# Side work of the DeltaNet projections: three places per product block instead of two, and the block inverses on one engine each

## The chip, the cores and the metric

One Trainium2 chip, and of it one core. The time is what the device takes for one execution, in microseconds. The kernel before ran three times: 3624.55, 3621.60 and 3624.28 us, median 3624.28.

## The reference, cut to what matters

A two-layer backbone over 1024 latent tokens and 256 context tokens, width 1024, float32. Layer 0 is an mLSTM and S5 mixer, layer 1 a bidirectional gated DeltaNet with 8 heads of 128; each is followed by a SwiGLU block. The change touches layer 1's mixer alone:

```
pc, pl = split(hc @ w_in), split(hl @ w_in)            # q, k, v, z and gates, 8 heads
qkv = silu(depthwise_conv3x3(...))                      # over a 64-column grid; the context is one row
q, k = l2norm(q) * scale, l2norm(k)
A   = strict_lower((k * beta) @ k.T * gamma)            # per chunk and head
sol = triangular_solve(A + I, [v * beta, k * beta * exp(G)])
attn = (q @ k.T) * gamma
S, (v_new, o_inter) = scan(step, 0, ...)                # the recurrence over the chunks
o = o_inter + attn @ v_new                              # both directions are added
y = rmsnorm(o) * silu(z) @ w_out
```

The kernel works with chunks of 128 tokens (10 of them: 2 context, 8 latent). The triangular solve becomes an explicit inverse of each 128x128 matrix: first of its 32x32 diagonal blocks, then of 64x64 and 128x128.

## The kernel before, in words

Every dense product runs three times in reduced precision (`mm3`, lines 124 to 126: high times high, high times low, low times high). `dense` makes one product block: 8 steps over the contraction, so 24 matmuls into one accumulator tile `pd`, for 256 (context, chunk 0) or 512 columns (chunks 1 and 2).

Layer 1's mixer has two stages. In the first, `layer1` calls `gdn_project` for the heads 0 to 7. For one head it makes the block of K (chunks 0, 1, 2), of Q (1, 2), for heads 0 to 5 that of the output gate z (`gdn_gate`, chunks 1 and 2), and of V (0, 1, 2). `conv_input` copies each product into an image, and `conv_block` does the 3x3 convolution there: line 1693 on ScalarE, lines 1695 on VectorE (8 taps of 751 ns for 512 columns), then the SiLU (lines 1697, 1698). The first K and Q blocks were made earlier. The gate blocks of heads 6 and 7 come last (`hw`).

**The side work of a head** is the generator `gdn_keys(h)`, started before the head's V block. It runs in pieces, from one `yield` to the next, and `pull(n)` runs n pieces at that place of the program. Its pieces: transposes of K (3) and Q (2) to token order with sums of squares (`to_tokens`: line 1710 on TensorE, 1713 and 1718 on ScalarE); the logarithms of the norms (line 1780 and `log_half`, lines 1530 to 1544, some 17 small VectorE steps that each need the one before) and from them the row factors `ei` (lines 1785 on VectorE, 1789 on ScalarE), written under `high_priority`; `K1` empty pieces; then the row parts `d_pr` (line 1821: TensorE transposes `ei`; lines 1822 to 1825: VectorE makes `rows` of it); `Y2` = 2 empty pieces; exponentials times Q (2 pieces, `d_qE`: TensorE 1843, ScalarE 1845, GpSimd 1847, stored by a DMA); then for three groups of chunks the decay factors (TensorE 1855 and 1857, ScalarE 1860) and the products K·K and K·Q (TensorE 1866 and 1878, GpSimd 1869, VectorE 1870 and 1881; 6 pieces), stored by DMAs; then V's transposes (3). Those are 18 pieces and K1 empty ones, and K0 more for head 0. With two places in a product block (one in its middle, one at its end) a head has 20 places: V 6, K 6, Q 4, gate 4. `set_side` first runs what is left of the old generator. For head 7 the pieces wait differently (L1, Y1, L2, K2).

**The 32x32 inverses** are `gdn_base(h0, nh)`: a load from `bl_dr`, 30 elimination steps, a masking at the end (lines 1929 to 1934) and a store to `bo_dr`. Each step has two halves, one per triangle, and each half is a product into `b_t` (lines 1920, 1924) and a sum into `b_x` (line 1926). The half r = 0 is on VectorE, r = 1 on GpSimd. It runs three times: heads 0 to 2 (written from head 4 on, one step per unit of the convolution), heads 3 to 5 (written after head 7), heads 6 and 7 (written in the second stage, heads 2 to 4). There is one buffer `b_x`.

In the second stage, `gdn_heads` runs the recurrence head by head (`gdn_recur`: TensorE 2073, 2081, 2104, VectorE 2075 and 2109, ScalarE 2085), with the next head's larger inverse (`gdn_inverse`) between its steps.

What sets the order: inside the mixer TensorE's instructions stay in program order (`in_pe_order`). Those of VectorE, ScalarE, GpSimd and the DMA issues are put in order by the framework, from a simulated timeline with priorities by program order (`high_priority` raises one by 400), and each engine then runs its own queue strictly in that order. So work that is written late but needs nothing late may stand early in a queue.

Of the kernel before, what the change touches and what calls it, by code (L numbers as in the profile page):

```python
# [16 lines left out]
P = 128  # L17
D = 1024
# [8 lines left out]
FFN = 2816  # L27
HP = 400
Y1, Y2 = 6, 2
K0, K1, K2 = 3, 3, 3  # L30
R0, R1, R2, R3 = 3,1,1,2
F1, F2 = 20,8
L1, L2 = 4,2
# [9 lines left out]
class Kernel:  # L43
# [84 lines left out]
    def dense(self, w, rhs, kb, n, c0=0, order=None, mid=0):  # L128


        ps = self.psd.tile([P, 512], F32, name="pd")
        for j, k in enumerate(order or range(kb)):
            if mid and j == kb // 2:
                self.pull(mid)
            self.mm3(ps[:, :n], (w[0][:, k, c0:c0 + P], w[1][:, k, c0:c0 + P]), rhs(k), j == 0, j == kb - 1)
        return ps[:, :n]
# [1518 lines left out]
    def conv_input(self, hs, w, img, chunks, mid=0):  # L1655

        nc = self.nc
        g, l = img
        for ci in chunks:
            t0, n = CHUNKS[ci]  # L1660
            ps = self.dense(w, lambda k: (hs[ci][0][:, k], hs[ci][1][:, k]), KB, n, mid=mid)
            if ci == 0:
                nc.scalar.copy(out=l[:, 1:1 + NCTX], in_=ps)
            else:
                r0 = 1 + (t0 - NCTX) // 64
                nc.scalar.copy(out=g[:, r0:r0 + n // 64, 1:65], in_=ps.rearrange("p (r c) -> p r c", c=64))
            self.pull(mid)

    def conv_block(self, hs, w0, blk, out, with_ctx, pool, mid=1):

        nc = self.nc
        g, l = img = self.img[self.nimg % 2]
        self.nimg += 1
        if blk not in self.early:
            w = self.load_w(self.ins["od_w_in"][0], 0, KB, w0)
            self.conv_input(hs, w, img, (0, 1, 2) if with_ctx else (1, 2), mid=mid)

        wc = lambda i: self.wcv[:, blk, i:i + 1]
        off = NCTX if with_ctx else 0
        units = [(out[:, 0:NCTX], (NCTX,), {i: l[:, i - 3:i - 3 + NCTX] for i in (4, 3, 5)})] if with_ctx else []  # L1680
        for hf in range(2):
            taps = {}
            for i in (4, 0, 1, 2, 3, 5, 6, 7, 8):
                dy, dx = divmod(i, 3)
                taps[i] = g[:, 8 * hf + dy:8 * hf + dy + 8, dx:dx + 64]
            units.append((out[:, off + 512 * hf:off + 512 * hf + 512], (8, 64), taps))
        for o, shape, taps in units:
            n = o.shape[-1]
            acc = self.psc.tile([P, 512], F32, name="cv_acc", tag="pc")[:, :n]
            a = acc.rearrange("p (r c) -> p r c", c=64) if len(shape) == 2 else acc  # L1690
            for i, src in taps.items():
                if i == 4:
                    nc.scalar.activation(out=a, in_=src, func=AF.Copy, scale=wc(4))  # L1693
                else:
                    nc.vector.scalar_tensor_tensor(out=a, in0=src, scalar=wc(i), in1=a, op0=ALU.mult, op1=ALU.add)  # L1695
            th = pool.tile([P, 512], F32, name="cv_th")
            nc.scalar.activation(out=th[:, :n], in_=acc, func=AF.Tanh, scale=0.5)
            nc.vector.scalar_tensor_tensor(out=o, in0=th[:, :n], scalar=1.0, in1=acc, op0=ALU.add, op1=ALU.mult)
            next(self.base, None)
# [21 lines left out]
    def gdn_gate(self, hs, hw, ci, qp, n=1):  # L1721

        nc = self.nc
        t0, nt = CHUNKS[ci]
        for h, w in hw:
            ps = self.dense(w, lambda k: (hs[ci][0][:, k], hs[ci][1][:, k]), KB, nt, mid=n)
            self.pull(n)
            zz = qp.tile([P, 512], F32, name="cv_th")
            nc.scalar.activation(out=zz, in_=ps, func=AF.Tanh, scale=0.5)
            nc.vector.scalar_tensor_tensor(out=zz, in0=zz, scalar=1.0, in1=ps, op0=ALU.add, op1=ALU.mult)  # L1730
            nc.sync.dma_start(out=self.z_dr[h, :, t0 - NCTX:t0 - NCTX + nt], in_=zz)
# [3 lines left out]

    LATE = 6

    def gdn_project(self, hs, h, tp, qp, kp):

        last = h == 7  # L1740
        kqv = [None] * 3
        def start():
            self.set_side(self.gdn_keys(h, kqv, kp, qp))
            self.pull()
        kT = tp.tile([P, T], F32, name="d_fT", bufs=3)
        self.conv_block(hs, D + h * P, 8 + h, kT, True, qp, 2 if last else 1)
        kqv[0] = kT
        self.nc.sync.dma_start(out=self.k_dr[h], in_=kT)
        qT = tp.tile([P, NLAT], F32, name="d_qT", bufs=2)
        if last:  # L1750
            start()
        self.conv_block(hs, h * P, h, qT, False, qp)
        kqv[1] = qT
        if h < self.LATE:
            w = self.gdn_gate_w(h)
            for ci in (1, 2):
                self.gdn_gate(hs, [(h, w)], ci, qp)
        vT = tp.tile([P, T], F32, name="d_fT", bufs=3)
        if not last:
            start()  # L1760
        self.conv_block(hs, 2 * D + h * P, 16 + h, vT, True, qp)
        kqv[2] = vT

# [139 lines left out]
            nc.gpsimd.affine_select(out=fb, in_=fb, pattern=[[-s, 32], [s, 32]], compare_op=ALU.is_ge, fill=0.0, base=0, channel_multiplier=0)  # L1903
        nc.gpsimd.tensor_copy(self.bm, f)

    def gdn_base(self, h0, nh, pool):

        nc = self.nc
        x = self.bx[:, 0]
# [1 line left out]
            nc.sync.dma_start(out=x[32 * b:32 * b + 10 * nh], in_=self.bl_dr[b, h0:h0 + nh].rearrange("h c j i -> (h c) j i"))  # L1911
        yield
        for j in range(1, 31):
            for r, e in ((0, nc.vector), (1, nc.gpsimd)):
                t = pool.tile([P, 256], F32, name=f"b_t{r}")
                m = 31 - j
                tv = t[:, :j * m]
                if r == 0:
                    tv = tv.rearrange("p (k i) -> p k i", i=m)
                    e.tensor_tensor(out=tv, in0=x[:, 0:j, j:j + 1].to_broadcast([P, j, m]), in1=x[:, j:j + 1, j + 1:].to_broadcast([P, j, m]), op=ALU.mult)  # L1920
                    d = x[:, 0:j, j + 1:]
                else:
                    tv = tv.rearrange("p (i k) -> p i k", k=j)
                    e.tensor_tensor(out=tv, in0=x[:, j + 1:, j:j + 1].to_broadcast([P, m, j]), in1=x[:, j:j + 1, 0:j].to_broadcast([P, m, j]), op=ALU.mult)
                    d = x[:, j + 1:, 0:j]
                e.tensor_tensor(out=d, in0=d, in1=tv, op=ALU.add)
            yield
# [224 lines left out]
    def layer1(self):  # L2152
# [40 lines left out]
        with s1:  # L2193
# [11 lines left out]
                self.ei3.append(t)  # L2205
            self.base = iter(())
            for h in range(8):
                if h == 4:
                    self.base = self.gdn_base(0, 3, bp)
                self.gdn_project(hs, h, tp, qp, kp)  # L2210
            for _ in self.base:
                pass
            self.base = self.gdn_base(3, 3, bp)
            next(self.base)
            hw = [(h, self.gdn_gate_w(h)) for h in range(self.LATE, 8)]
            self.gdn_gate(hs, hw, 1, qp, G1)
            self.gdn_places()
# [22 lines left out]
    def gdn_heads(self, bp, sb):  # L2240
# [16 lines left out]
        for h in range(8):  # L2257
            with self.tc.high_priority(offset=HP):
                next(finish, None)
            if h < 7:  # L2260
                with self.tc.issue_after(self.blocks_dma.ins):
                    tn = self.gdn_load(h + 1, (d0, d1)[(h + 1) % 2])
                if h == 1:
                    for _ in base:
                        pass
                    base = self.gdn_base(6, 2, bp)
                    with self.tc.issue_after(tn["dma"].ins):
                        next(base)
                inv = self.gdn_inverse(h + 1, tn)
# [120 lines left out]
```

## Time and profile before

| | |
|---|---|
| median of 3 runs | 3624.28 us |
| profiled execution | 3625.0 us, of it the traced span 3623.3 us |
| busy in the span | TensorE 3368.1, weight loads 2788.7, VectorE 1904.1, ScalarE 1003.9, GpSimd 954.2 us |
| mean granted TensorE clock | 0.966 |
| first stage (projections) | about 1875 to 2430 us of the span |
| second stage (recurrence) | about 2470 to 2780 us |

"Busy" of TensorE is modelled and holds no idle time; time at half clock counts as busy. PE is TensorE, PEld its weight loads, DVE VectorE, ACT ScalarE, POOL GpSimd. Outside the two stages, layer 0 and the SwiGLU blocks fill the span.

### The profile page before, as it was taken

What the parts mean: (1) busy time and instruction counts of PE and PEld (TensorE: products, weight loads), DVE (VectorE), ACT (ScalarE), POOL (GpSimd) and SP (SyncE); (2) the same over time, 40 slices, a digit from 0 to 9 for tenths busy, and PEclk for the clock granted to TensorE, in tenths of its full rate; (3) what the DMA queues carried; (4) which work ended last, traced back from release to release, by engine and by line L of the source; (5) the groups of instructions that cost most, each with busy time, mean ns of one, the idle gap of its engine ahead of it and who ended that gap; (6) DMA issues with size and microseconds to landing.
All of it is one profiled execution on the core that took longest, in us unless ns stands there. A gap on an engine that the chain in (4) does not pass through costs nothing. (4 is left out here: it accounts for less than half of the span.)

```text
span 3623.3 us, 48343 instructions
## 1 busy us (share of the span) xinstructions
PE 3368.1 (93%) x18527; PEld 2788.7 (77%) x18527; DVE 1904.1 (53%) x4084; ACT 1003.9 (28%) x2409; POOL 954.2 (26%) x783
## 2 busy tenths in 40 slices
PE   6999978999999999999988979788899999999998
PEld 4787667886777778888777767567897788888888
DVE  6659967444333333333467797885754432222224
ACT  3221135331111111111244535443444211111112
POOL 1111124141111111111342352444543222222223
PEclk7999989999999999999999989899999999999999
DMA  7553575512222221111123333246553011111111
GB/s 241 130 168 122 165 213 147 178 59 89 92 81 75 77 76 53 41 35 41 59 63 95 114 117 119 89 131 205 154 183 134 24 45 52 48 48 51 43 53 65
DMA packets 396828, 360.31 MB, mean 99 GB/s; under 512 B 104763, under 2 KB 329755, under 8 KB 396086
## 3 DMA queue, kind: packets, MB, share of 16 engines
q1 hardware_dynamic: 396598, 357.23, 31.9%
q8 instruction: 146, 2.39, 0.3%
q14 instruction: 84, 0.69, 0.1%
HBM read 258.92 MB, written 96.75 MB: 98 GB/s over the span
## 5 line engine op out<-in xcount | busy, mean ns | idle before, releaser
L124 PE MATMUL pd<-hh,w_hi 128*128 128x512 f32 (+1 forms) x3064 | 1156.0, 378 | 3.9 <-ACT hh L284 3.3
L125 PE MATMUL pd<-hl,w_hi 128*128 128x512 f32 (+1 forms) x3064 | 1137.7, 371 | 3.0 <-DVE hl L276 2.9
L126 PE MATMUL pd<-hh,w_lo 128*128 128x512 f32 (+1 forms) x3064 | 1131.8, 371 | 1.6 <-POOL w_lo L118 1.5
L118 POOL TENSOR_TENSOR w_lo<-w_raw,w_hi 128x1024 fp32r<-128x1024 f32 (+2 forms) x205 | 479.2, 2338 | 2004.3 <-ACT w_hi L117 1930.8
L124 PEld LDWEIGHTS pd<-hh,w_hi 128*128 128x128 f32 x3064 | 588.5, 192 | 116.6 <-issue 8.6
L126 PEld LDWEIGHTS pd<-hh,w_lo 128*128 128x128 f32 x3064 | 586.8, 192 | 108.2 <-issue 2.9
L125 PEld LDWEIGHTS pd<-hl,w_hi 128*128 128x128 f32 x3064 | 588.3, 192 | 103.1 <-DVE hl L276 6.0
L117 ACT CAST w_hi<-w_raw 128x1024 fp32r<-128x1024 f32 (+2 forms) x205 | 207.6, 1012 | 964.4 <-PE pd L125 750.1
L1337 DVE SCALAR_TENSOR_TENSOR x<-pd,mod,x 128x512 f32<-128x512 f32 (+1 forms) x408 | 267.5, 670 | 267.1 <-PE pd L126 266.8
L1325 DVE TENSOR_TENSOR ntmp<-ntmp,pd 128x512 f32<-128x512 f32 (+1 forms) x110 | 69.8, 634 | 508.2 <-PE pd L126 507.9
L124 PE MATMUL pd<-g_hi,w_hi 128*128 128x512 f32 (+1 forms) x844 | 314.3, 373 | 0.6 <-DVE x L1337 0.6
L125 PE MATMUL pd<-g_lo,w_hi 128*128 128x512 f32 (+1 forms) x844 | 307.1, 364 | 0.0
L126 PE MATMUL pd<-g_hi,w_lo 128*128 128x512 f32 (+1 forms) x844 | 302.4, 364 | 0.6 <-POOL w_lo L118 0.6
L1695 DVE SCALAR_TENSOR_TENSOR cv_acc<-img,wcv,cv_acc 128x512 f32<-128x512 f32 x384 | 278.6, 751 | 39.6 <-ACT cv_acc L1693 26.8
L1324 DVE SCALAR_TENSOR_TENSOR ntmp<-ntmp,pd 128x512 f32<-128x512 f32 (+1 forms) x110 | 69.7, 634 | 269.9 <-ACT ntmp L1323 268.2
L124 PEld LDWEIGHTS pd<-g_hi,w_hi 128*128 128x128 f32 x844 | 159.2, 189 | 49.3 <-issue 21.4
L1326 ACT ACTIVATE g_hi<-ntmp 128x512 fp32r<-128x512 f32 (+1 forms) x110 | 64.7, 588 | 441.9 <-DVE ntmp L1325 441.5
L126 PEld LDWEIGHTS pd<-g_hi,w_lo 128*128 128x128 f32 x844 | 158.3, 188 | 28.7 <-issue 2.1
L125 PEld LDWEIGHTS pd<-g_lo,w_hi 128*128 128x128 f32 x844 | 159.4, 189 | 23.1
L1327 DVE SCALAR_TENSOR_TENSOR g_lo<-ntmp,g_hi 128x512 fp32r<-128x512 f32 (+1 forms) x110 | 139.7, 1270 | 68.2 <-ACT g_hi L1326 68.2
L245 POOL TENSOR_TENSOR nacc<-nacc,ntmp 128x256 f32<-128x256 f32 (+1 forms) x72 | 74.5, 1040 | 125.2 <-ACT ntmp L241 123.6
L189 PE MATMUL a_ps<-a_raw,svec 128*32 128x256 f32 x768 | 84.4, 435 | 19.3 <-DMA a_raw<-in_ada_w_dram 19.3
(542 smaller groups left out, 4535.6 us busy)
## 6 DMA issues: line engine op xcount, KB each, us to landing
w_raw<-in_ffn_w_dram SPq DMA_DIRECT2D x106, 512.0 KB
a_raw<-in_ada_w_dram SPq DMA_DIRECT2D x96, 512.0 KB
w_raw<-in_od_w_in_dram SPq DMA_DIRECT2D x32, 512.0 KB
w_raw<-in_ffn_w_dram SPq DMA_DIRECT2D x32, 384.0 KB
w_raw<-in_ev_w_in_dram SPq DMA_DIRECT2D x20, 512.0 KB
x_dr<-x SPq DMA_DIRECT2D x4, 2048.0 KB
p_dr<-mp_t SPq DMA_DIRECT2D x32, 256.0 KB
x<-x_dr SPq DMA_DIRECT2D x16, 512.0 KB
```

The source lines that it names most:

```text
L117: nc.scalar.copy(out=hi, in_=raw)
L118: self.w_lo_engine.tensor_tensor(out=lo, in0=raw, in1=hi.bitcast(F32), op=ALU.subtract)
L124: mm(ps, lh, rh, start=first, stop=False)
L125: mm(ps, lh, rl, start=False, stop=False)
L126: mm(ps, ll, rh, start=False, stop=last)
L189: nc.tensor.matmul(ps[32 * j:32 * j + 32, :256], self.svec[:, k], raw[:, j * 256:(j + 1) * 256], start=(k == 0), stop=(k == KB - 1), tile_ ...
L245: nc.gpsimd.tensor_tensor(out=acc, in0=acc, in1=sq, op=ALU.add)
L1324: nc.vector.scalar_tensor_tensor(out=th[:, :n], in0=th[:, :n], scalar=1.0, in1=p1, op0=ALU.add, op1=ALU.mult)
L1325: nc.vector.tensor_tensor(out=th[:, :n], in0=th[:, :n], in1=p3, op=ALU.mult)
L1327: nc.vector.scalar_tensor_tensor(out=gl[:, t0:t0 + n], in0=th[:, :n], scalar=0.5, in1=gh[:, t0:t0 + n].bitcast(F32), op0=ALU.mult, op1=ALU ...
L1337: nc.vector.scalar_tensor_tensor(out=xd, in0=ps, scalar=g, in1=xd, op0=ALU.mult, op1=ALU.add)
L1695: nc.vector.scalar_tensor_tensor(out=a, in0=src, scalar=wc(i), in1=a, op0=ALU.mult, op1=ALU.add)
```

## The change

- `K0, K1` go from 3, 3 to 4, 7.
- `dense` takes a tuple of steps at which to pull a piece; for a tuple of m places, m - 1 more are pulled at the block's end. With (3, 5) a product block has three places: before step 3, before step 5, at its end. K, Q, gate and V of the heads take it. The K block of head 7 takes (2, 3, 5, 6): seven pieces per product block (four before).
- `gdn_base` gets its engine: heads 0 to 2 and 3 to 5 wholly on GpSimd, heads 6 and 7 wholly on VectorE. The masking at the end stays on VectorE.
- The inverses of heads 0 to 2 are written from the V block of head 3 on (before: from head 4), those of heads 3 to 5 from the V block of head 7 on (before: after it), with two steps at each gate block of heads 6 and 7.

```diff
--- before.py
+++ after.py
@@ -27,7 +27,7 @@
 FFN = 2816
 HP = 400
 Y1, Y2 = 6, 2
-K0, K1, K2 = 3, 3, 3
+K0, K1, K2 = 4, 7, 3
 R0, R1, R2, R3 = 3,1,1,2
 F1, F2 = 20,8
 L1, L2 = 4,2
@@ -130,7 +130,9 @@
 
         ps = self.psd.tile([P, 512], F32, name="pd")
         for j, k in enumerate(order or range(kb)):
-            if mid and j == kb // 2:
+            if isinstance(mid, tuple):
+                self.pull(mid.count(j))
+            elif mid and j == kb // 2:
                 self.pull(mid)
             self.mm3(ps[:, :n], (w[0][:, k, c0:c0 + P], w[1][:, k, c0:c0 + P]), rhs(k), j == 0, j == kb - 1)
         return ps[:, :n]
@@ -1664,9 +1666,9 @@
             else:
                 r0 = 1 + (t0 - NCTX) // 64
                 nc.scalar.copy(out=g[:, r0:r0 + n // 64, 1:65], in_=ps.rearrange("p (r c) -> p r c", c=64))
-            self.pull(mid)
-
-    def conv_block(self, hs, w0, blk, out, with_ctx, pool, mid=1):
+            self.pull(len(mid) - 1 if isinstance(mid, tuple) else mid)
+
+    def conv_block(self, hs, w0, blk, out, with_ctx, pool, mid=(3, 5)):
 
         nc = self.nc
         g, l = img = self.img[self.nimg % 2]
@@ -1724,7 +1726,10 @@
         t0, nt = CHUNKS[ci]
         for h, w in hw:
             ps = self.dense(w, lambda k: (hs[ci][0][:, k], hs[ci][1][:, k]), KB, nt, mid=n)
-            self.pull(n)
+            self.pull(len(n) - 1 if isinstance(n, tuple) else n)
+            if h >= self.LATE:
+                next(self.base, None)
+                next(self.base, None)
             zz = qp.tile([P, 512], F32, name="cv_th")
             nc.scalar.activation(out=zz, in_=ps, func=AF.Tanh, scale=0.5)
             nc.vector.scalar_tensor_tensor(out=zz, in0=zz, scalar=1.0, in1=ps, op0=ALU.add, op1=ALU.mult)
@@ -1735,7 +1740,7 @@
 
     LATE = 6
 
-    def gdn_project(self, hs, h, tp, qp, kp):
+    def gdn_project(self, hs, h, tp, qp, kp, bp):
 
         last = h == 7
         kqv = [None] * 3
@@ -1743,7 +1748,7 @@
             self.set_side(self.gdn_keys(h, kqv, kp, qp))
             self.pull()
         kT = tp.tile([P, T], F32, name="d_fT", bufs=3)
-        self.conv_block(hs, D + h * P, 8 + h, kT, True, qp, 2 if last else 1)
+        self.conv_block(hs, D + h * P, 8 + h, kT, True, qp, (2, 3, 5, 6) if last else (3, 5))
         kqv[0] = kT
         self.nc.sync.dma_start(out=self.k_dr[h], in_=kT)
         qT = tp.tile([P, NLAT], F32, name="d_qT", bufs=2)
@@ -1754,10 +1759,15 @@
         if h < self.LATE:
             w = self.gdn_gate_w(h)
             for ci in (1, 2):
-                self.gdn_gate(hs, [(h, w)], ci, qp)
+                self.gdn_gate(hs, [(h, w)], ci, qp, (3, 5))
         vT = tp.tile([P, T], F32, name="d_fT", bufs=3)
         if not last:
             start()
+
+        if h in (3, 7):
+            for _ in self.base:
+                pass
+            self.base = self.gdn_base(0 if h == 3 else 3, 3, bp, self.nc.gpsimd)
         self.conv_block(hs, 2 * D + h * P, 16 + h, vT, True, qp)
         kqv[2] = vT
 
@@ -1903,7 +1913,7 @@
             nc.gpsimd.affine_select(out=fb, in_=fb, pattern=[[-s, 32], [s, 32]], compare_op=ALU.is_ge, fill=0.0, base=0, channel_multiplier=0)
         nc.gpsimd.tensor_copy(self.bm, f)
 
-    def gdn_base(self, h0, nh, pool):
+    def gdn_base(self, h0, nh, pool, e):
 
         nc = self.nc
         x = self.bx[:, 0]
@@ -1911,9 +1921,9 @@
             nc.sync.dma_start(out=x[32 * b:32 * b + 10 * nh], in_=self.bl_dr[b, h0:h0 + nh].rearrange("h c j i -> (h c) j i"))
         yield
         for j in range(1, 31):
-            for r, e in ((0, nc.vector), (1, nc.gpsimd)):
+            m = 31 - j
+            for r in range(2):
                 t = pool.tile([P, 256], F32, name=f"b_t{r}")
-                m = 31 - j
                 tv = t[:, :j * m]
                 if r == 0:
                     tv = tv.rearrange("p (k i) -> p k i", i=m)
@@ -2205,13 +2215,7 @@
                 self.ei3.append(t)
             self.base = iter(())
             for h in range(8):
-                if h == 4:
-                    self.base = self.gdn_base(0, 3, bp)
-                self.gdn_project(hs, h, tp, qp, kp)
-            for _ in self.base:
-                pass
-            self.base = self.gdn_base(3, 3, bp)
-            next(self.base)
+                self.gdn_project(hs, h, tp, qp, kp, bp)
             hw = [(h, self.gdn_gate_w(h)) for h in range(self.LATE, 8)]
             self.gdn_gate(hs, hw, 1, qp, G1)
             self.gdn_places()
@@ -2263,7 +2267,7 @@
                 if h == 1:
                     for _ in base:
                         pass
-                    base = self.gdn_base(6, 2, bp)
+                    base = self.gdn_base(6, 2, bp, nc.vector)
                     with self.tc.issue_after(tn["dma"].ins):
                         next(base)
                 inv = self.gdn_inverse(h + 1, tn)
```

## Rows read from the trace of the kernel before

**Rows 1.** Two stretches: busy PE, PEld, DVE, ACT, POOL (count); clock, DMA share, GB/s.
```profile
1880.00:2440.00 560.00, 465.90 (x2526) 385.97 (x2527) 467.80 (x861) 263.02 (x775) 219.34 (x225) 0.92 0.35 109
...
2515.00:2590.00 75.00, 62.53 (x468) 57.41 (x468) 62.81 (x157) 25.61 (x93) 53.44 (x82) 0.98 0.40 114
```

**Rows 2.** Waits of TensorE, 1880:2095, 2095:2430, 2340:2430: us in total, times, longest.
```profile
PE d_pr L1821 <- ACT ei L1789: 15.8, 3, 6.0
...
PE d_pr L1821 <- ACT ei L1789: 47.8, 4, 20.9
...
PE d_pk L1866 <- DVE d_ca L1870: 3.9, 1, 3.9
PE d_pE L1843 <- DVE rows L1825: 1.3, 1, 1.3
```

**Rows 3.** Timeline of TensorE, head 2: start us, us, instruction [idle before it <- releaser].
```profile
2036.11 0.60 PE L1710 MATMUL tt_ps<-ident,d_qT 128*128 128x128 f32 x4
...
2044.79 0.28 PE L126 MATMUL pd<-hh,w_lo 128*128 128x256 f32 x1
2049.99 0.48 PE L1821 MATMUL d_pr<-ident,ei 128*128 128x128 f32 x1 [4.92 <-ACT ei L1789]
```

**Rows 4.** The same view's columns as rows 1, stretches after waits.
```profile
2345.80:2362.70 16.90, 11.49 (x72) 9.00 (x71) 16.26 (x25) 7.87 (x21) 14.24 (x16) 1.00 0.12 47
2050.10:2055.50 5.40, 5.40 (x14) 4.24 (x15) 5.21 (x12) 0.55 (x2) 0.00 (x0) 0.50 0.00 0
2134.20:2137.50 3.30, 3.29 (x9) 2.61 (x10) 3.18 (x10) 1.07 (x4) 0.20 (x1) 0.50 0.00 0
```

**Rows 5.** Timeline of VectorE, head 2: the logarithms' first and last steps.
```profile
2038.88 0.18 DVE L1780 TENSOR_SCALAR d_ss<-d_ss 128x18 f32<-128x18 f32 x1 [0.33 <-ACT tt_sq L1718]
...
2049.00 0.21 DVE L1785 TENSOR_TENSOR d_e<-dg_pre,d_lkq 128x60 f32<-128x60 f32 x1
```

**Rows 6.** Timelines of TensorE and VectorE, head 3.
```profile
2104.31 0.60 PE L1710 MATMUL tt_ps<-ident,d_qT 128*128 128x128 f32 x4
...
2134.21 0.48 PE L1821 MATMUL d_pr<-ident,ei 128*128 128x128 f32 x1 [20.94 <-ACT ei L1789]
...
2111.84 0.62 DVE L1780 TENSOR_SCALAR d_ss<-d_ss 128x18 f32<-128x18 f32 x1
```

**Rows 7.** Busy time while head 3's logarithms run: all engines; line 1920; line 1926.
```profile
2111.80:2133.80 22.00, 1.47 (x13) 1.27 (x11) 22.00 (x49) 2.14 (x4) 19.73 (x32) 0.62 0.09 24
...
2111.80:2133.80 22.00, 3.94 (x6) 0.62 0.09 24
...
2111.80:2133.80 22.00, 2.57 (x7) 8.94 (x16) 0.62 0.09 24
```

**Rows 8.** Timeline of TensorE, head 6.
```profile
2342.60 0.48 PE L1821 MATMUL d_pr<-ident,ei 128*128 128x128 f32 x1 [16.99 <-ACT ei L1789]
```

**Rows 9.** Instructions of tile b_x: duration ns min/median/max, first and last start, forms.
```profile
L1920 DVE TENSOR_TENSOR b_t<-b_x x90: 191/392/2462, 2093.5 to 2563.5; 128x30 f32<-128x30 f32 x6, 128x58 f32<-128x58 f32 x6, 128x84 f32<-128x84 f32 x6, 128x108 f32<-128x108 f32 x6
L1924 POOL TENSOR_TENSOR b_t<-b_x x90: 235/539/781, 2093.5 to 2580.5; 128x30 f32<-128x30 f32 x6, 128x58 f32<-128x58 f32 x6, 128x84 f32<-128x84 f32 x6, 128x108 f32<-128x108 f32 x6
L1926 DVE TENSOR_TENSOR b_x<-b_x,b_t x90: 190/390/1410, 2093.7 to 2563.7; 128x30 f32<-128x30 f32 x6, 128x58 f32<-128x58 f32 x6, 128x84 f32<-128x84 f32 x6, 128x108 f32<-128x108 f32 x6
L1926 POOL TENSOR_TENSOR b_x<-b_x,b_t x90: 249/578/927, 2093.9 to 2580.8; 128x30 f32<-128x30 f32 x6, 128x58 f32<-128x58 f32 x6, 128x84 f32<-128x84 f32 x6, 128x108 f32<-128x108 f32 x6
```

**Rows 10.** Lines 1869, 1860 in 1880:2440, columns as rows 9; one ScalarE wait.
```profile
L1869 POOL TENSOR_TENSOR d_ca<-d_e,d_e x23: 722/1272/1408, 1938.7 to 2438.9; 128x512 f32<-128x512 f32 x15, 128x256 f32<-128x256 f32 x8
...
L1860 ACT ACTIVATE d_e<-d_pe,d_e x152: 349/380/429, 1936.7 to 2438.4; 128x128 f32<-128x128 f32 x152
...
ACT d_qE L1845 <- DMA q_dr<-d_qE: 19.9, 12, 2.6
```

**Rows 11.** Waits of TensorE in 2470:2590 and 2430:2470, columns as rows 2.
```profile
PE e_pk L2073 <- DVE e_S L2109: 6.1, 8, 1.1
...
PE d_pe L1855 <- ACT d_e L1860: 3.9, 1, 3.9
```

## The prediction

> **What bounds the kernel now.** I read the busy times by stretch first. In the projection stage no engine is full: of 560 us TensorE is busy 465.9, VectorE 467.8, ScalarE 263.0, GpSimd 219.3, and the clock is 0.92 [rows 1]. So I went to the waits of TensorE, whose order is fixed. One line dominates: the row parts `d_pr`, waiting for `ei`, cost 15.8 us in three waits and 47.8 us in four, 63.6 us in all [rows 2]; other waits there are a few us each. The reader is to see that this one has a known length. In head 2 the second half of Q's transposes starts at 2036.11; TensorE then has the 512-column block of V and the 256-column block of the next K to do, is finished at 2044.79 + 0.28 = 2045.07, and idles 4.92 us until 2049.99 [rows 3]. Meanwhile VectorE works off the chain of logarithms: from 2038.88 to 2049.21 [rows 5], 10.3 us for some 17 small steps, because taps of the convolution stand between them. From transposes to row parts it is 13.88 us, and TensorE has work for 8.96.
>
> The wait costs a second time: for 5.4 us after it the granted clock is 0.50, the 1.2 GHz level, so some 2.7 us are lost [rows 4]. After the long waits of heads 3 and 6 the low stretch that follows is 3.3 us [rows 4].
>
> Heads 3 and 6 wait 20.94 and 16.99 us [rows 6, 8]; the other five share 63.6 - 37.9 = 25.7 us, so about 5 each. What is special in head 3: VectorE is busy for all 22.0 us of the chain, and 3.94 + 2.57 = 6.5 us of it are block-inverse work, while GpSimd is busy 19.7 of 22 [rows 7]. The chain also starts late: the first step comes 7.5 us after the transposes began (2104.31 to 2111.84), in head 2 after 2.8 [rows 5, 6]. And a small step beside GpSimd's work lasts 0.62 us in place of 0.18 [rows 5, 6]. These inverses ran long before the place where the program writes them: VectorE's and GpSimd's order is planned, and they are put wherever their input allows.
>
> **The change part by part.**
>
> (a) Places. The logarithms stand behind piece 5, the row parts behind K1 more pieces. Before, pieces 1 to 5 end at V's second block's end, and the row parts are piece 9, the end of the next K's 256-column block. With three places per block, piece 5 is at step 3 of V's second block, and with K1 = 7 the row parts are piece 13: again the end of that 256-column block. So the row parts stay, and the transposes and the logarithms move forward by 5/8 of a 512-column block. The 8.96 us are 1.5 such blocks, so a block is about 5.8 us (8.6 us of products without the transposes, 5.75) and the gain is 3.6 us. TensorE then has 12.5 us of work against 13.9: the five ordinary waits shrink from 25.7 to 5 x 1.4 = 7. **Term: -19.** Bounds: 0 (the planner starts the chain no earlier) to -25.7 (all hidden).
>
> (b) Clock. A wait of 1.3 us [rows 2] lies in a stretch whose granted clock stayed 1.00 [rows 4], so I take it that five waits of 1.4 us no longer bring the 0.50: 5 x 2.7. **Term: -13.5**, bounds -13.5 and 0.
>
> (c) VectorE's half of the inverses goes, in this stage, to GpSimd: 60 instructions per group at 0.39 us, 23 us by the medians [rows 9], twice. VectorE then has about 420 us in place of 467.8. In head 3's chain the 6.5 us go, and most of the late start (I take 3 of 4.7 us); the small steps stay lengthened, for GpSimd is busy there still longer. 29.9 us from transposes to row parts become 20.4, against 12.5 us of work: 8 us are left. Head 6 I treat alike: 37.9 us become 16. **Term: -22**, bounds 0 and -37.9. The clock after two waits of 8 us is as after head 2's, 2.7 each in place of 1.65: **+2**. The wait of `d_pk` for VectorE's `d_ca` (3.9 us, head 6 [rows 2]) falls in the time of head 6's inverses and should go with them, with a little clock: **-5**, bounds 0 and -7.
>
> (d) What GpSimd takes on: per group 120 instructions at 0.54 to 0.58, so 67 us where it has 34 [rows 9]. GpSimd has 219 of 560 us filled [rows 1], so 66 us more fit by sum. But in the 70 to 80 us after each load its queue is full, and the adds for `d_ca` (1.27 us [rows 10]), the products for `d_qE` and the low halves of the weights stand in the same queue. If the plan puts them behind inverse steps that last longer than planned, TensorE waits for a bank. Bounds: 0, and the extra 33 us per group passed on in full, +66. I take **+5**, as most of this work is not urgent and no such wait shows when GpSimd was busy 19.7 of 22 us.
>
> (e) The denser places. From the exponentials on, two pieces used to have one 512-column block (5.75 us) between them; now they have 3.8 us on average. One group of four chunks needs 8 exponentials of 0.38, then GpSimd's 1.27 and VectorE's `d_ca` before its bank is free: about 5.5 us with its own matmuls running beside it for some 3 [rows 10]. That just fits, with little left; and ScalarE already waits 19.9 us in 12 times for the stores of `d_qE` [rows 10], which come closer together. I take 1.2 us for each of seven heads: **+8**. Bounds: 0, and 6 us of wait with 3 us of clock for each, +63. The gate blocks are left without side work. The stores (keys, `q_dr`, `ca_dr`, `bl_dr`, `at_dr`, V) and the inverses' four loads and stores each are as many as before and go past the weight loads of the same SyncE queue a few us earlier; with the DMA engines at 0.35 [rows 1] I cost that at nothing; if a weight load came late behind them, it would be its issue time, below 1 us each.
>
> (f) The last heads. In head 7's K block all of head 6's remaining pieces run, seven per block; the exponentials now pile up behind the first, 256-column block: **+3** (0 to +12). Head 7's own pieces come earlier, so fewer are drained without products beside them; there `d_pe` waited 3.9 us [rows 11]: **-4** (0 to -8).
>
> (g) Heads 6 and 7's inverse, wholly on VectorE, beside the recurrence. VectorE is busy 62.8 of 75 us there [rows 1], 120 instructions at 0.39 instead of 60 add 23 us, and TensorE's waits on VectorE's `e_S` (6.1 us in 8 times, the main one [rows 11]) are the ones at risk. The plan gives the recurrence priority, so the extra work stretches over later heads. **+3**, bounds -5 (fewer collisions with GpSimd) and +16. Here a rule speaks for the lower end. Base instructions of one kind last from 191 to 2462 ns on VectorE [rows 9]. The Trainium skill, "SBUF — State Buffer", section "Who interferes with whom", says that a VectorE instruction with two inputs in SBUF and a GpSimd instruction that reads SBUF exclude each other: the second stands still until the first is done. By it one engine alone would do its steps faster than either did beside the other, and (g) would be about 0 and the sum 3 us better; but by the same rule the logarithms of heads 3 and 6 stay slowed for longer, so I leave the sum as it is.
>
> **Sum:** -19 - 13.5 - 22 + 2 - 5 + 5 + 8 + 3 - 4 + 3 = -42.5 us, made against the profiled execution: 3625.0 us, of which 3623.3 are the span. The median of the runs is 0.7 us lower, 3624.3, so I forecast 3582 us.
>
> **The rivals.**
>
> *All of it is hidden.* If VectorE, freed of the inverses, runs the chain without falling behind anywhere, all seven waits and their low clock go: -63.6 - 17 - 5, with +12 for the rest, is -74: 3551 us. For it: VectorE would be at some 85% of a shorter stage. Against: 17 dependent steps take 10.3 us even where no inverse runs [rows 5].
>
> *The chain does not move.* The logarithms have raised priority already; if the plan lets taps of the convolution in front of them, piece 5 earlier brings nothing, (a) and (b) fall out, and what is left is (c) to (g): -42.5 + 32.5 = -10, or, with half of the shift working, -26. I put this case at 3605 us. For it: head 3's chain started 7.5 us after its transposes. Against: in head 2 it started as soon as ScalarE's sums were there (released by `tt_sq` after 0.33 us [rows 5]).
>
> *GpSimd becomes the bound.* (d) at some 25 us per group instead of 2.5: 3582 + 45 = 3627 us, no change. It decides where a `d_ca` add or a weight's low half stands behind some 40 inverse steps.
>
> *The denser places cost more than the chain gave: slower.* At 9 us per head in (e) in place of 1.2, +55: 3637 us. Its place is between the exponentials and the last K·Q product of each head, with three banks for the side work; it decides from 7 us per head on, where the sum is zero. For it: 3.8 us between pieces against a chain of 5.5. Against: TensorE shows almost no such wait now, but with 5.75 us.
>
> **How the numbers follow.** Forecast 0.43 (its own spread 3565 to 3600); all hidden 0.14; chain does not move 0.20; GpSimd the bound 0.11; slower by density 0.12. A difference under 0.2% (7 us) counts as none, being what a measurement of this kernel can tell. Forecast and all-hidden are faster; of the third nearly all (0.19); of GpSimd's case 0.03 faster, 0.05 same, 0.03 slower; of the last 0.02 same, 0.10 slower; the remaining 0.01 is same. Faster 0.79, same 0.08, slower 0.13. For 8 times in 10 the range leaves out part of the all-hidden case and most of the slower one: 3552 to 3630.
>
> **What would show it.** In the profile of the changed kernel: `d_pr`'s wait for `ei` in total near 23 us, with five waits between 0 and 2 and two near 8; the clock of the projection stage 0.95 or more; no base instruction on VectorE before the recurrence, and GpSimd near 285 us there; new waits of `d_pe`, `d_pk`, `tt_ps` for `d_e` and `d_ca` near 1 us per head; in the recurrence waits for `e_S` and `e_rr` within a few us of now. I am wrong if `d_pr` still waits some 5 us in the ordinary heads, if waits of 4 us and more appear behind line 1869 or 1845, or if GpSimd's `w_lo` holds up product blocks.

## The result, and the profile after

The changed kernel takes 3599.45 us (median of four runs, 3597.30 to 3600.71), the kernel before 3623.57 beside it: ratio 0.9934 [0.9916, 0.9951], 24 us or 0.67% faster. Measured once more, in five further runs beside nine of the kernel before, it took 3600.27 us against 3626.52: 0.9931 [0.9916, 0.9945]. The forecast was 3582 us and a gain of 42.5 us, so the direction was right and the gain little more than half of it.

Runs of one kernel differ by some 10 us, in one case by 18, and part of that lies ahead of the projections: the two profiled executions of the changed kernel differ by 8.0 us, and their first token transposes start at 1882.2 and 1888.6 us (1883.4 and 1885.0 before). So the stages are compared by themselves. The first runs from the first `tt_ps` (token transpose) of TensorE in this mixer to the first `e_pu` (a product of the recurrence), the second from there to the last `e_pu`. For each, "idle" is the sum of TensorE's gaps over 60 ns, and "lost" half of the time at the 0.50 clock in which TensorE was not idle. Each row is worked out from one trace; the edits are explained with the experiments:

```
kernel (profiled execution)   first stage  idle   lost   second stage  idle  lost
before                          585.1     100.8   26.2      310.0      28.6   7.6
before, again                   581.8      98.1   25.6      308.8      27.4   7.5
after                           553.1      72.0   23.9      315.8      29.4  12.0
after, again                    554.8      74.1   23.0      315.6      29.3  12.2
e1_places                       569.7      82.3   29.5      308.4      28.5   5.7
e2_inverses                     567.9      84.7   26.1      314.3      29.6   9.0
e2_again                        575.8      94.5   23.6      313.4      28.8   9.7
e3_one_buffer                   548.1      66.9   23.7      313.8      31.6   6.8
e4_rows_later                   554.5      74.2   20.7      314.9      28.2  11.1
e5_last_split                   552.5      71.0   24.2      308.2      28.5   5.7
e6_together                     532.1      56.7   16.6      308.5      28.9   5.7
e7_k_block                      522.9      50.4   13.5      308.0      27.0   6.8
```

So the change took 27 to 32 us from the first stage and put 6 to 7 on the second. What follows takes 844 to 845 us in every kernel. Two executions of one kernel differ by 1.7 to 7.9 us in the first stage and by 0.2 to 1.2 us in the second, so a smaller difference between two rows shows nothing.

The lines move by ten in the changed kernel (`d_pr` 1821 is 1831, `d_pE` 1843 is 1853, `ei` 1789 is 1799) and by two below 1730. TensorE's waits in the first stage, the view of [rows 2]:

```profile
PE d_pE L1853 <- DVE rows L1835: 19.6, 6, 8.6
PE d_pr L1831 <- ACT ei L1799: 19.3, 4, 5.8
PE tt_ps L1712 <- DVE d_fT L1700: 9.3, 3, 3.7
PE tt_ps L1712 <- DVE d_qT L1700: 7.2, 3, 3.9
PE tt_ps L1712 <- ACT tt_sq L1720: 4.0, 4, 1.3
...
PE d_pe L1865 <- ACT d_e L1870: 3.6, 4, 1.3
```

The 63.6 us of `d_pr` are 19.3. On top stands a wait that hardly existed: the exponentials `d_pE` wait for `rows`, 1.3 us in one head before, 19.6 us in six heads now.

Busy time by stretch, answering to [rows 1] (the same part of the program; columns PE, PEld, DVE, ACT, POOL, clock, DMA share, GB/s):

```profile
1880.00:2406.00 526.00, 460.67 (x2524) 381.40 (x2525) 420.30 (x742) 263.87 (x777) 263.10 (x344) 0.94 0.37 114
2481.00:2556.00 75.00, 60.95 (x428) 54.30 (x429) 67.47 (x212) 23.88 (x85) 21.77 (x20) 0.95 0.39 108
```

VectorE's 467.8 us are 420.3 (forecast about 420), GpSimd's 219.3 are 263.1 (forecast near 285), and the clock of 0.92 is 0.94 (forecast 0.95 or more). Head 2 on TensorE, answering to [rows 3]:

```profile
2040.91 0.28 PE L126 MATMUL pd<-hh,w_lo 128*128 128x256 f32 x1
2041.03 0.27 PE L1831 MATMUL d_pr<-ident,ei 128*128 128x128 f32 x1
...
2046.62 0.55 PE L1853 MATMUL d_pE<-rows,sel 128*128 128x128 bf16 x7 [1.90 <-DVE rows L1835]
```

The 4.92 us ahead of `d_pr` are gone; 1.90 us stand ahead of `d_pE`. The reason is on VectorE, answering to [rows 5]:

```profile
2032.47 0.18 DVE L1790 TENSOR_SCALAR d_ss<-d_ss 128x18 f32<-128x18 f32 x1 [3.04 <-ACT tt_sq L1720]
...
2036.82 0.21 DVE L1795 TENSOR_TENSOR d_e<-dg_pre,d_lkq 128x60 f32<-128x60 f32 x1
...
2041.79 0.28 DVE L1832 CAST rows<-d_pr 128x128 bf16<-128x128 f32 x1
...
2046.27 0.30 DVE L1835 TENSOR_TENSOR rows<-d_pr,rows 32x128 bf16<-32x128 f32 x1
```

The logarithms take 4.6 us (2032.47 to 2037.03) where they took 10.3: VectorE had run dry and waited 3.04 us for ScalarE, and only 3 taps stand between them, against 9 before. The four steps that make `rows` still end 5.5 us after `d_pr` starts, with taps between them, and TensorE now comes back after 5/8 of a block, 3.6 us.

Head 6, answering to [rows 8], is the strangest part. On VectorE:

```profile
2293.21 11.20 DVE L1790 TENSOR_SCALAR d_ss<-d_ss 128x18 f32<-128x18 f32 x1 [2.08 <-ACT tt_sq L1720]
2304.45 0.18 DVE L1532 TENSOR_SCALAR ln_m<-d_ss 128x18 int32<-128x18 int32 x1
```

On GpSimd at the end of that time:

```profile
2302.00 0.61 POOL L1934 TENSOR_TENSOR b_t<-b_x 128x234 f32<-128x234 f32 x1
2302.56 1.24 POOL L1936 TENSOR_TENSOR b_x<-b_x,b_t 128x234 f32<-128x234 f32 x2
2303.76 0.63 POOL L1930 TENSOR_TENSOR b_t<-b_x 128x238 f32<-128x238 f32 x1
2309.95 2.35 POOL L118 TENSOR_TENSOR w_lo<-w_raw,w_hi 128x1024 fp32r<-128x1024 f32 x1 [5.57 <-ACT w_hi L117]
```

And on TensorE, with the granted clock of the stretch behind it (columns as above), which answers to [rows 4]:

```profile
2307.53 0.47 PE L1831 MATMUL d_pr<-ident,ei 128*128 128x128 f32 x1 [5.36 <-ACT ei L1799]
...
2318.52 1.76 PE L1853 MATMUL d_pE<-rows,sel 128*128 128x128 bf16 x15 [8.59 <-DVE rows L1835]
```

```profile
2307.40:2327.70 20.30, 10.57 (x47) 8.50 (x48) 15.53 (x26) 9.21 (x21) 14.41 (x18) 0.50 0.18 56
```

The first small step on VectorE, 0.18 us elsewhere, lasts 11.20 us, as long as GpSimd's instructions follow each other with no gap (each starts about 0.05 us before the one ahead is through), and ends within 0.02 us of GpSimd's going idle at 2304.39. In head 3 the same step lasts 7.10 us and ends at 2105.04, where GpSimd's last instruction ends at 2105.01.

### The profile page after: what moved, and what is told of

It reads as the page before. It is cut to its first block, busy times and chain, and to the rows that moved or that the text cites. A ratio compares the mean times of both kernels' runs of the same rounds, so it can differ in the third digit from the quotient of the medians.

```text
span 3595.6 us, 48351 instructions
## 1 busy us (share of the span) xinstructions
PE 3364.7 (94%) x18527; PEld 2788.5 (78%) x18527; DVE 1868.4 (52%) x4024; ACT 1005.4 (28%) x2409; POOL 970.6 (27%) x843
## 3 DMA queue, kind: packets, MB, share of 16 engines
q8 instruction: 146, 2.39, 0.3%
```

## The experiments

**The parts alone.** e1_places is the changed kernel with the inverses as before; e2_inverses is the kernel before with the inverses of the change.

Against the changed kernel, e1_places is

```diff
-            if h >= self.LATE:
-                next(self.base, None)
-                next(self.base, None)
...
-        if h in (3, 7):
-            for _ in self.base:
-                pass
-            self.base = self.gdn_base(0 if h == 3 else 3, 3, bp, self.nc.gpsimd)
...
-            for r in range(2):
+            for r, e in ((0, nc.vector), (1, nc.gpsimd)):
...
+                if h == 4: self.base = self.gdn_base(0, 3, bp, None)
...
+            for _ in self.base: pass
+            self.base = self.gdn_base(3, 3, bp, None); next(self.base)
...
-                    base = self.gdn_base(6, 2, bp, nc.vector)
+                    base = self.gdn_base(6, 2, bp, None)
```

and e2_inverses is the kernel before with just these lines as the change has them, each group on its one engine.

> The three places per block, K0 and K1 of the change, with the block inverses as before (VectorE and GpSimd, written where they were). Theory A (the gain comes from the places: the logarithms of the ordinary heads move 5/8 of a block ahead; the inverses on GpSimd alone bring little, because their back-to-back instructions shut VectorE's small steps out, 7.1 and 11.2 us for one step in heads 3 and 6): most of the 24 us is here, 3597 to 3605 us; the ordinary heads' d_pr wait is gone and d_pE waits 1.9 us for rows, as after the change; heads 3 and 6 wait about 17 and 13 us. Rival B (VectorE's relief from the inverses makes the gain): 3610 to 3620 us.

> The inverses on one engine each and written earlier, with two places per block and K0 = K1 = 3 as before. Theory A: the five ordinary heads keep their 4.9 us d_pr waits and the 0.5 clock after them; heads 3 and 6 gain little, with one VectorE step of several us shut out in their chains: 3612 to 3624 us. Rival B: heads 3 and 6 lose most of their 38 us of wait: 3595 to 3606 us.

Measured: e1_places 3611.12 us, 0.9969 [0.9957, 0.9981]; e2_inverses 3620.75 us, 0.9994 [0.9985, 1.0004]. The places alone bring 11 us, less than theory A said, and the inverses alone nothing that can be told from zero; together they bring 24 to 26. The time of e1_places lies in rival B's range and that of e2_inverses in theory A's, so neither theory had this. TensorE's waits in the first stage, first of e1_places, then of e2_inverses (sum, times, longest):

```profile
PE d_pE L1853 <- DVE rows L1835: 19.9, 6, 10.1
PE d_pr L1831 <- ACT ei L1799: 15.4, 4, 5.9
...
PE d_pe L1865 <- DVE d_ca L1880: 8.2, 4, 3.8
```

```profile
PE d_pr L1829 <- ACT ei L1797: 55.8, 7, 13.5
```

In the ordinary heads 1, 2, 4 and 5 the gain at `d_pr` is the places' alone. There e1_places waits for nothing, and its logarithms in head 2 take 4.6 us, as after the change, though the inverses are as before:

```profile
2035.74 0.18 DVE L1790 TENSOR_SCALAR d_ss<-d_ss 128x18 f32<-128x18 f32 x1 [3.04 <-ACT tt_sq L1720]
...
2040.09 0.21 DVE L1795 TENSOR_TENSOR d_e<-dg_pre,d_lkq 128x60 f32<-128x60 f32 x1
```

e1_places gains at `d_pr` in the other heads too, even without the move of the inverses (heads 3 and 6 wait 5.95 and 1.94 us there, against 17 and 13 expected), and loses at `rows` in head 6 (10.1 us) and at `d_ca`, where inverse steps stand in VectorE's queue. In e2_inverses heads 3 and 6 wait 12.6 and 9.0 us instead of 20.9 and 17.0, but head 4 waits 13.5 instead of 4.9: on GpSimd the inverses last longer (86 us for heads 0 to 2, against 53), and their masking on VectorE (2.07 and 2.11 us) and a step held up for 2.37 us beside a `w_lo` of 2.44 us on GpSimd fall into head 4's logarithms. With the earlier places head 4 waits for nothing at `d_pr`, with the inverses as before or as the change has them. That is one place where the two parts help each other, 8.6 us; it is read from the traces and was not tried by itself. How large their interplay is stays open: by the medians the parts add up to some 13 us and the whole brings 24 to 26, but by the stages of the table (means of two executions where there are two) they add up to 22 us and the whole brings 23.

The profile of e2_inverses had a first stage 17 us shorter than before, against a median 1.4 us lower, so it ran again:

> The inverses alone once more: in its profile the first stage was 17.2 us shorter than before and the second 4.3 longer, while the median was only 1.4 us lower. Theory A (the profiled stages are right, and its medians carry the some us by which the part ahead of the first stage differs between executions): first stage 566 to 570 us again, and a median 8 to 16 us below the kernel before. Rival: the first stage itself varies in this kernel, 575 us or more this time, and the median is again within 3 us.

> The kernel before, profiled a second time. Theory A: first stage 585 us and second stage 310 us within 3 us; the start of the first stage differs by up to 8 us. Rival: a stage differs by 10 us.

Measured: e2_again 3620.82 us, 0.9992 [0.9983, 1.0001], its first stage 575.8 us. The rival holds: in this kernel the first stage itself differs by 8 us between executions (the `d_pk` waits of the last heads and the `tt_ps` waits of the first and last do), and the medians decide. The kernel before gave 581.8 and 308.8 us in before_again, 3.3 and 1.2 us less than at first: the first stage just outside theory A's 3 us, the second within them, and far from the rival's 10.

**Why a small step lasts 11 us.** e3_one_buffer gives both halves of a step the same product buffer, so that each instruction waits for the one before:

```diff
-                t = pool.tile([P, 256], F32, name=f"b_t{r}")
+                t = pool.tile([P, 256], F32, name="b_t")
```

> The change, with one product buffer b_t for both halves of an inverse step, so that each of GpSimd's (and for heads 6 and 7 VectorE's) instructions waits for the one before it. Theory A (VectorE's small step is shut out because GpSimd's instructions follow each other without a gap): the first logarithm step of heads 3 and 6, 7.1 and 11.2 us long after the change, is back under 1.5 us; their d_pr and rows waits (6.6 and 14 us) fall by about half; 3585 to 3594 us. Rival C (those steps are long for another reason, such as a wait for ScalarE's sums counted as duration): they stay over 5 us and the time stays within 3 us of 3599.

Measured: 3596.71 us, 0.9928 [0.9916, 0.9941]; first stage 548.1 us. Head 6 on VectorE and on GpSimd:

```profile
2302.62 0.18 DVE L1790 TENSOR_SCALAR d_ss<-d_ss 128x18 f32<-128x18 f32 x1 [2.08 <-ACT tt_sq L1720]
2302.83 0.46 DVE L1532 TENSOR_SCALAR ln_m<-d_ss 128x18 int32<-128x18 int32 x1
...
2307.20 0.22 DVE L1795 TENSOR_TENSOR d_e<-dg_pre,d_lkq 128x60 f32<-128x60 f32 x1
```

```profile
2302.16 0.51 POOL L1934 TENSOR_TENSOR b_t<-b_x 128x168 f32<-128x168 f32 x1
2302.74 0.51 POOL L1936 TENSOR_TENSOR b_x<-b_x,b_t 128x168 f32<-128x168 f32 x1
```

GpSimd now leaves some 0.07 us between its instructions (2302.16 + 0.51 to 2302.74), and VectorE's step slips in: 0.18 us, the next one 0.46, the whole chain 4.8 us where it took 14. Theory A holds for the mechanism: the same work on the same engines, only the gaps are new, and `d_pr` of heads 3 and 6 waits no longer (19.3 to 9.8 us in all). With `rows` the two heads wait 8.9 us in place of 20.5. But no gain in time is clear of the noise: the ratio is 0.9928 where the changed kernel has 0.9934 and 0.9931, so 1 to 2 us, against 5 to 14 us expected (this run was on another chip than the changed kernel's later runs, so the ratios to the kernel before are compared). The first stage is 5 to 7 us shorter, which is no more than two executions of e2_inverses differ. One reason is that the inverses last longer and now reach head 4, where two masking steps of 1.96 and 1.90 us stand between VectorE's steps for `rows` and TensorE waits 5.7 us:

```profile
PE d_pE L1853 <- DVE rows L1835: 20.4, 6, 5.7
...
PE d_pr L1831 <- ACT ei L1799: 9.8, 2, 4.9
```

**The stretch from row parts to exponentials.** e4_rows_later has one more empty piece there:

```diff
-Y1, Y2 = 6, 2
+Y1, Y2 = 6, 3
```

> The change with Y2 = 3: the exponentials come one place later, a whole block after the row parts as before the change. Theory A (the shorter stretch from row parts to exponentials cost 19.6 us of d_pE waits for rows in six heads): these waits fall under 5 us in total, 3585 to 3594 us. Rival D (VectorE only falls behind somewhere else): as much wait appears at d_pe, d_pk or tt_ps, within 3 us of 3599.

Measured: 3596.93 us, 0.9930 [0.9918, 0.9942].

```profile
PE d_pr L1831 <- ACT ei L1799: 27.3, 5, 12.4
...
PE d_pE L1853 <- DVE rows L1835: 8.8, 2, 7.7
```

In heads 1, 2, 4 and 5 the wait for `rows` is gone, as theory A has it; heads 3 and 6 keep 1.1 and 7.7 us, with their shut-out steps (7.6 and 8.9 us), so the total is 8.8 and not under 5. And `d_pr` waits 8 us more, above all in head 7 (12.4 in place of 5.9 us) and head 4 (3.3 us, where there was none), and the first stage is no shorter. By the ratio, 0.9930, no gain can be told from zero. So for this edit by itself rival D is right in kind, though the wait came back at `d_pr` and not where it said.

**The second stage.** The changed kernel ran again beside the next three kernels (after_again), and e5_last_split gives the two halves of the inverse of heads 6 and 7 to VectorE and GpSimd again:

```diff
+        es = (e, e) if e else (self.nc.vector, self.nc.gpsimd)
...
-            for r in range(2):
+            for r, e in enumerate(es):
...
-                    base = self.gdn_base(6, 2, bp, nc.vector)
+                    base = self.gdn_base(6, 2, bp, None)
```

> The changed kernel once more, on the chip of the next three runs, to see how much one execution differs from another. Theory A: the first stage (first token transposes to the first e_pu) is 553 us and the second 316 us within 3 us, and only what lies before the first stage moves by some us. Rival: the stages themselves vary by 10 us, and single profiles can't be compared.

> The change, with the inverse of heads 6 and 7 split between VectorE and GpSimd as before. Theory A (120 VectorE instructions beside the recurrence made the second stage 5.8 us longer): the second stage, 310.0 us before and 315.8 after, is back at 308 to 311, the whole 4 to 6 us faster than the change. Rival E (the second stage is longer because the first ends earlier, so loads and the weights of what follows are late): it stays at 315 to 316.

Measured: after_again has stages of 554.8 and 315.6 us, within 1.7 us of the first profile, as its theory A has it. e5_last_split took 3594.37 us, 0.9912 [0.9897, 0.9927], and its second stage 308.2 us against 315.6. Theory A holds: one engine for that group costs 7.4 us, of which 0.8 are idle time (29.3 to 28.5) and 6.5 half clock (12.2 to 5.7). The table bears it out: the second stage is 313.4 to 315.8 us in all kernels with that group on VectorE alone and 308.0 to 310.0 us in all with the split. From 2440 to 2720 us TensorE's waits for VectorE are longer after the change than in e5_last_split (sum, times, longest; the changed kernel first):

```profile
PE e_pu L2091 <- DVE e_rr L2085: 6.2, 7, 1.8
```

```profile
PE e_pu L2091 <- DVE e_rr L2085: 5.1, 6, 1.2
```

The longest wait for `e_S` there is 1.7 us in place of 1.3. Behind the waits of 1.8 and 1.7 us the granted clock is 0.50 for 3.4 us each.

**All cures at once.** e6_together has one buffer for the inverses on GpSimd, Y2 = 3 for heads 0 to 6, the split of e5, and a fourth edit that did not run by itself: for head 7 the row parts come two pieces later. Without the lines of the split it is

```diff
-        for _ in range(K1 if together else Y1):
+        for _ in range(K1 if together else 8):
...
-        for _ in range(Y2):
+        for _ in range(3 if together else Y2):
...
-            for _ in range(L2):
+            for _ in range(0):
...
-                t = pool.tile([P, 256], F32, name=f"b_t{r}")
+                t = pool.tile([P, 256], F32, name=f"b_t{0 if es[0] is es[1] else r}")
```

and e7_k_block besides spreads head 6's side work in head 7's K block anew, with other places for each chunk (the lines that pick a chunk's places are left out):

```diff
-        self.conv_block(hs, D + h * P, 8 + h, kT, True, qp, (2, 3, 5, 6) if last else (3, 5))
+        self.conv_block(hs, D + h * P, 8 + h, kT, True, qp, {0: (3, 5), 1: (3, 5, 7), 2: (1, 3, 4, 5, 6)} if last else (3, 5))
...
```

> The three cures at once: one product buffer for the inverses on GpSimd, Y2 = 3 for heads 0 to 6, the inverse of heads 6 and 7 split; and for head 7 the row parts two pieces later (Y1 = 8, L2 = 0), whose wait was 5.9 us. Theory A (the terms are separate places of one fixed order, so they add): the first stage 535 to 543 us, the second 308 to 311, the whole 3577 to 3588 us. Rival D (VectorE's queue is what is full, and a wait taken away comes back later): first stage 546 us or more, 3590 us or more.

> As the run before, and in head 7's K block the side work of head 6 spread anew: row parts at the end of the 256-column block, the exponentials 5/8 of a 512-column block later, the rest in the last block. Theory A: head 6's d_pr and rows waits (14 us after the change, 5.5 with one buffer) fall under 3 us, against 2 to 4 us of new waits of d_pe and d_pk where the rest is dense: 2 to 5 us faster than the run before. Rival D: no faster, since the dense end waits for ScalarE's exponentials and for banks as long.

Measured: e6_together 3571.99 us, 0.9854 [0.9835, 0.9873]; e7_k_block 3565.09 us, 0.9832 [0.9818, 0.9847], on the same chip as the changed kernel's 3600.27. Two of the waits of e7_k_block:

```profile
PE d_pr L1831 <- ACT ei L1799: 8.5, 2, 4.9
PE tt_ps L1712 <- DVE d_fT L1700: 8.4, 3, 3.7
```

`d_pE` for `rows` is down to 2.3 us (5.7 in e6_together, 4.0 of it in head 6, which e7_k_block brings to 0.5); what is left of `d_pr` is head 0 (4.9) and head 7 (3.6). Together the four edits give 28 us, where e5 alone gave 6 and e3 and e4 alone nothing clear of the noise. The traces show why: the wait that one of them uncovered is the one that another takes away. The 5.7 us for `rows` in head 4 of e3 are 0.7 in e6_together, and the 3.3 and 12.4 us at `d_pr` in heads 4 and 7 of e4 are 0 and 3.9. Since the edit for head 7 was not tried alone, its own share of the 28 us is not known. Rival D is wrong for the whole, and theory A's sum was too small: the first stage is 532.1 us where it said 535 to 543, the time 5 us below its range. e7_k_block is 6.9 us faster than e6_together, where 2 to 5 were expected, 1.7% faster than the kernel before and 1.0% faster than the changed one.

## Why the prediction was right or wrong, step by step

(a) *Right about the shift, lucky in the size.* The five ordinary heads' waits fell from 25.7 to 4.9 us (head 0 alone), forecast 7. In head 2 TensorE's work from transposes to row parts went from 8.96 to 12.21 us, forecast 12.5. With the old 13.88 us between them that would have left 1.7 us, forecast 1.4. But the chain also got shorter, 4.6 us for 10.3, and so the wait is gone in four heads; it stays in head 0, where the logarithms still take 14.8 us. The argument against "all is hidden", that 17 steps take 10.3 us even without inverses, took the taps between them for a property of the chain; e1_places shows that the new places alone take them away. Part of the 10.3 us was the lock-out too. The three steps of line 1543 in head 2 of the kernel before, the third of them 2.38 us long beside a `w_lo` of 2.39 us on GpSimd:

```profile
2042.81 2.81 DVE L1543 SCALAR_TENSOR_TENSOR ln_p<-ln_p,ln_a 128x18 f32<-128x18 f32 x3
```

After the change three of them take 0.60 us.

(b) *Mis-sized.* Forecast were -13.5 and, in (c), +2 at the clock; "lost" fell by 2.3 (26.2 to 23.9). The stretches at 0.50 after `d_pr` went in heads 1, 2, 4 and 5, but new ones came with new waits: 20.3 us in head 6, and 3.4 us after the 1.9 us waits of heads 2 and 5 (after those of heads 1 and 4 the clock stayed at 1.00).

(c) *Right in direction, and incomplete.* `d_pr` of heads 3 and 6: 37.9 to 8.6 us (3.2 and 5.4), forecast 16; `d_pk` for `d_ca`, 3.9 us, went. The late start in head 3 went whole, where 3 of 4.7 us were taken: its first step waited for ScalarE's sums alone. But "the small steps stay lengthened" meant 0.62 us for 0.18, and one step was 7.1 and 11.2 us.

(d) *Right that in the first stage TensorE waits for none of GpSimd's results; wrong about the price.* It came by the other way: VectorE shut out. In the second stage one such wait is new, 2.0 us of `e_py` for `e_out`.

(e) *The step that failed.* "The denser places" were costed from the exponentials on, and there nothing was lost: `d_pe` and `d_pk` wait less than before (12.3 to 4.8 us). What the prediction didn't look at is the stretch ahead of them, from the row parts to the exponentials, where Y2 = 2 pieces went from one block to 5/8. In (a) it counted that the row parts stay and what stands before them moves; what stands behind them moves too. `rows` needs 5.5 us, TensorE leaves 3.6: 1.9 us in each of four heads, 3.4 and 8.6 in heads 3 and 6. e4_rows_later shows the first by itself: with a whole block there, the four heads wait for nothing. Heads 3 and 6 need more than the longer stretch or the gaps alone (8.8 and 8.9 us are left); with both, in e6_together, they wait 0.9 and 4.0. The term was +8 and is +17.4 at `d_pE`, and +5.2 at the token transposes (16.3 to 21.5), where waits for ScalarE's `tt_sq` (4.0 us in four heads) and for `d_qT` in head 6 (3.9 us) are new: they now come closer together or earlier than ScalarE and VectorE are ready. No experiment took these apart.

(f) *Wrong for head 7's row parts, right for its end.* The row parts, which waited for nothing, wait 5.9 us. The likely reason is that their distance is counted in pieces, and three places per block run through it sooner; with two pieces more, in e6_together, they wait 3.9, beside three other edits. The pile-up of head 6's exponentials (+3) is 1.0 us at `d_pe`, and the drained `d_pe` wait went from 3.9 to below 1, as forecast.

(g) *Right in kind, mis-sized:* +3 forecast, +5.8 and +6.8 measured, and e5_last_split shows it by itself. The Trainium skill's rule of "SBUF — State Buffer", "Who interferes with whom", which would have made this term about 0, does hold in the length of the steps: VectorE's inverse steps of the second stage take 0.39 us on average alone, 0.52 with the split. But 120 of them fill 46 us of VectorE's time where 60 filled 31, and the second stage did not gain from keeping them off GpSimd.

In sum the first stage was forecast 45.5 us shorter and is 27 to 32; of its idle time `d_pr` gave back 44.3, and `d_pE` and `tt_ps` took 22.6. The terms as measured add up to the 32.0 us of the first two profiles within 1 us: -20.7 in (a), -2.3 in (b), -29.4 at `d_pr` in (c), -7.5 at `d_pe` and `d_pk`, +17.4 and +5.2 in (e), +5.9 in (f).

## What to carry to other kernels

Where one engine's order is fixed and others answer to it, a distance is what is bought: a step that moves forward gains distance to what reads it and loses as much to what it reads, so every link of the chain (here logarithms, row parts, rows, exponentials) needs its own check of engine time against queue time. Waits in such an order hide each other: two cures that brought nothing clear of the noise alone, one that brought 6 us and a fourth untried alone brought 28 together, so a cure isn't to be dropped for bringing little alone. And GpSimd work beside a critical chain of small VectorE steps did least harm here with gaps between its instructions, for without them a step stood still.

## What the runs showed of the hardware that was not expected

A VectorE step of 0.18 us was held up for 7.1 and 11.2 us by a run of GpSimd instructions with no gap between them, and ended when GpSimd went idle (2304.41 against 2304.39 us, and 2105.04 against 2105.01). With 0.07 us between GpSimd's instructions the same step took 0.18 us and its successors up to 0.5. The Trainium skill, "SBUF — State Buffer", section "Who interferes with whom", has the second instruction stand still until the first is done; here the trace differs, for the wait outlasted some twenty instructions. The prediction quotes that section for VectorE instructions with two inputs in SBUF; this step, a TENSOR_SCALAR, has one, and the section names such steps too, for a mode that takes both ports, which no view here shows. The convolution's taps (one input in SBUF, the other in PSUM) kept 0.72 to 0.76 us beside the inverses on GpSimd.
